# Columns of their own for the low parts' sums: five matmuls a block in place of six

## The chip, the cores and the metric

The kernel runs on one core of one Trainium2 chip. The metric is device time in microseconds (us) of one launch, taken as the median of the runs. Its engines appear below as PE (TensorE matmuls), PEld (TensorE weight loads), DVE (VectorE), ACT (ScalarE), POOL (GpSimd) and SP (SyncE, which here starts the transfers).

## The reference

The kernel computes one step of a decoder layer for 512 tokens of a prompt and 8 samples of one token each, 520 tokens in all, with 1024 features. Cut to its products:

```
h      = rmsnorm(x) * (1 + scale) + shift
proj   = h @ w_in                        # 1024 -> S5 input u | z | xBC | dt | gate_s5 | gate_ssd
ya     = gelu(s5(u));  ya = ya * sigmoid(ya @ w_glu + b_glu)
yb     = rmsnorm(ssd(conv(xBC), dt) * silu(z))          # 2048 features
merged = sigmoid(gate_s5) * (ya @ w_branch_s5) + sigmoid(gate_ssd) * (yb @ w_branch_ssd)
x     += gate * rmsnorm(merged @ w_out)
h      = rmsnorm(x) * (1 + scale_f) + shift_f
g, v   = split(h @ w_ffn_in)             # 2 x 2816
x     += gate_f * rmsnorm((silu(g) * v) @ w_ffn_out)
```

It also returns the new states of both state-space branches and of the convolution. All data are float32.

## The kernel before

Features lie on the partitions and tokens in the columns. A weight tile gives 128 output features. The 520 tokens are two halves of 260 (HT), since a PSUM bank holds 512 columns of sums. The input's 1024 features are 8 blocks of 128 (bssd has 16 blocks, fo has 22).

To keep the precision, each operand is held as a high and a low part, both of the type float32r (the profile's fp32r). A block is then three products: high by high and low input by high weights, and high input by low weights. `product` (L1148) issues them for a block, six matmuls of 260 columns into the tile's PSUM pair:

```
1152        for n in halves:
1154            self.mm(p[n][:, :s.stop - s.start], wh, xh[:, s], start=start, stop=False)
1155            self.mm(p[n][:, :s.stop - s.start], wh, xl[:, s], start=False, stop=False)
```

and then, for both halves, the high input with `wl`. Each matmul loads its 128 x 128 weights anew.

The main stream goes through the weight tiles in the order u, dt, gates, B, C, xs, z, then glu (8 tiles), bs5 (8), bssd (8), wo, fg and fu (gate and value of the second branch, 22 each), fo (8). wo and the first four fg and fu go by halves of the tokens, and so do the last two fo; the other 18 fg and 18 fu and the first six fo take both halves at once. The tiles use two PSUM pairs, pm0 and pm1, in turn. Four further banks serve the side work (the S5 and SSD branches, norms, states).

When a tile's sums are complete, `evac` (L1376) takes them out of pm: fg by a SiLU on ACT, fu by a product on DVE with the SiLU's result and a split in high and low part (ACT cast, DVE subtraction), fo by `mix_in` (L1561) with ACT, the others by copies, sigmoids and products. The weights for a tile two ahead are split meanwhile: ACT casts `whi`, DVE subtracts into `wlo`; of both there are three buffers in turn. From about 845 us on, the side work `ssd_state` renews the 8 samples' states: loads (in_ssm), products on DVE, stores.

No operation is issued at once. Every helper (`mm` L716, `acp` L694 for ACT copies, `vtt` L639 for DVE products and sums, `dma` L712) records an operation with an estimated cost in a `Plan`, which then searches for a good order by list scheduling with some random tries. All matmuls thus have line 722, all DVE products line 640, all ACT copies line 696. DVE and ACT take their operations strictly in the order found.

The end of the kernel: the last two fo tiles by halves (cut at 264 tokens, `cutp`), the last deviations in `rstd_last` (L1645, 256 tokens with a token a partition), `finish` (L1621) for the output.

Of the kernel before, what the change touches and what calls it, by code (L numbers as in the profile page):

```python
# [16 lines left out]
NP, NS = 512, 8  # L17
T = NP + NS
HT = T // 2
KD = 8  # L20
# [29 lines left out]
class Root:  # L50
    """A tile: `get` gives the real one (it may be made late); `loc` names the memory it lies in."""
# [14 lines left out]
class Ap:  # L66
    """A view of a tile: its shape and addresses at once, the real view when the operation is issued."""
# [110 lines left out]
# delay in us from the end of an operation to the start of one that waits for it  # L178
# [7 lines left out]
class Line:  # L186
    """The time of one engine: busy stretches, into whose gaps operations are put."""
# [24 lines left out]
class Plan:  # L212
    """Records operations with the memory they touch, and orders them for the engines."""
# [51 lines left out]
    def remake(self, loc, fn, words):  # L265
        """The memory `loc` gets a new tile: after everything that used the old one."""
# [8 lines left out]
    def order(self):  # L275
        """The best of some schedules: by the longest way to the end, then by latest starts."""
# [38 lines left out]
    def back(self):  # L315
        """Priorities from the schedule played backwards: the time from an operation's latest start to the end."""
# [35 lines left out]
    def play(self):  # L352
        """The course of the operations, each engine taking the most urgent of those that can start."""
# [69 lines left out]
    def shift(self, t, free, cand):  # L423
        """An operation of DVE that ACT may take at time t, where that is done sooner."""
# [32 lines left out]
class Arena:  # L457
    """One run of words in a tile of one type; blocks are cut out of it first fit."""
# [39 lines left out]
class Mem:  # L498
    """A fixed float32 arena, and slots whose type (float32 or float32r) is chosen when one is empty."""
# [10 lines left out]
    def find(self, n, dt, top):  # L510
        """The place for n words: an arena index (0 = the fixed one), or None."""
# [89 lines left out]
class Builder:  # L601
    def __init__(self, tc, I, O, sb, ps, dr):
# [10 lines left out]
        self.cutp = HT  # L613
# [6 lines left out]
        self.sg, self.ffh, self.ffl = {}, [], []  # L620
# [57 lines left out]
    def relu(self, o, a, s):  # L678
        """max(a + s, 0)"""
# [18 lines left out]
    def dma(self, o, a, boost=0.0):  # L698
        """Starts a transfer; returns the estimate of its end."""
# [25 lines left out]
    def idle(self, o, n, after=None):  # L725
        """Matmuls on zeros."""
        z = self.hi[:, KD - 1]
# [4 lines left out]
    def tp(self, o, a, n):  # L732
        d = self.ident[:n, :n]
        self.pe(.108, lambda: self.nc.tensor.transpose(real(o), real(a), real(d)), [o], [a, d])  # L734
# [8 lines left out]
    def bunch(self):  # L743
        """Matmuls that have to follow one another (sums that are open in one bank)."""
# [10 lines left out]
    def main(self):  # L755
        """The matmuls gathered in `group`, as one operation of the main stream."""
# [24 lines left out]
    def can(self, sizes, dt=F32, spare=0):  # L781
        """Whether the blocks fit, with room for `spare` token rows beside them."""
# [13 lines left out]
    def wblk(self, sizes, spare=2, dt=F32, prio=2):  # L796
        """Blocks for side work; a request that waits holds back those of less urgent work."""
# [88 lines left out]
    def ahead(self, j, table, f):  # L886
        """Prepares the weights of the use j of a chunk, unless that is done."""
# [3 lines left out]
    def split(self, hi, lo, src):  # L891
# [8 lines left out]
    def build(self):  # L900
# [4 lines left out]
        self.hi, self.lo = [rt(KD * T, n).rearrange("p (k t) -> p k t", k=KD) for n in ("hi", "lo")]  # L905
# [22 lines left out]
        # weight stream  # L928
# [30 lines left out]
        # half of the tokens at a time where the next step waits for all features  # L959
# [15 lines left out]
        # startup: modulation for the mixer, first norm  # L975
# [36 lines left out]
        # the first three tiles advance with the scale, two feature blocks at a time  # L1012
        b23 = [self.banks.pop() for _ in range(2)]
        ps = [[self.pm[0][:, n] for n in both], [self.pm[1][:, n] for n in both], b23]
        if NDUM:
            # matmuls on zeros: they keep the array busy, and so its clock at the full rate, until there are data
            self.mset("G", f_(self.hi[:, KD - 1]), 0.0)
            self.idle(b23[1], NDUM)
        for k in range(KD):
# [24 lines left out]
            for i in range(3):  # L1044
                self.product(*self.wt[i][:2], k, ps[i], both, k == 0, k == 7, self.hi[:, k], self.lo[:, k])
# [24 lines left out]
        for ti, (kind, idx, chs, m, halves) in enumerate(tiles[3:]):  # L1070
# [4 lines left out]
            else:  # L1075
                if self.nhalf == 0:
                    while len(self.banks) < 2:
                        self.tick()
                        self.now += 0.3
                    self.ring4 = [self.pm[0][:, 0], self.banks.pop(), self.pm[1][:, 0], self.banks.pop()]  # L1080
                if kind == "fo" and idx == 8 - NLAST and halves[0] == 0:
                    self.evac(*pend)
                    pend = None
                    self.cutp = T - 256
# [7 lines left out]
            nk, rhs = self.rhs(kind)  # L1092
            for k in range(nk):
# [8 lines left out]
                else:  # L1102
                    self.product(hi, lo, kk, pn, halves, k == 0, k == nk - 1, *rhs(k))
                if (kind, idx) == last:
                    if k == 0:
                        self.gelu()
                    self.split(self.hi[:, k], self.lo[:, k], self.ub.v(KD, T)[:, k])
                if (kind, idx) == ("glu", 7) and k < 7:
# [3 lines left out]
                    self.split(self.hi[:, k], self.lo[:, k], self.ub.v(KD, T)[:, k])  # L1112
                if (kind, idx) == ("bssd", 7):
                    self.ygh[k].free()
                    self.ygl[k].free()
# [28 lines left out]
    def span(self, n):  # L1144
        """The tokens of half n."""
        return slice(n * self.cutp, n * T + (1 - n) * self.cutp)

    def product(self, hi, lo, k, p, halves, start, stop, xh, xl):  # L1148
# [3 lines left out]
        for n in halves:  # L1152
            s = self.span(n)
            self.mm(p[n][:, :s.stop - s.start], wh, xh[:, s], start=start, stop=False)
            self.mm(p[n][:, :s.stop - s.start], wh, xl[:, s], start=False, stop=False)
        for n in halves:
            s = self.span(n)
            self.mm(p[n][:, :s.stop - s.start], wl, xh[:, s], start=False, stop=stop)
        self.main()

    def dt_mm(self, k, p, w):
        """The 32 columns of dt, high and low parts side by side, summed later."""
        self.group = []
        for n in range(2):
            for i, x in enumerate((self.hi, self.lo)):
                self.mm(p[:64, n, :HT], w[:, 64 * k:64 * k + 64], x[:, k, n * HT:(n + 1) * HT],
# [6 lines left out]
    def rhs(self, kind):  # L1173
        if kind == "bssd":
            return 16, lambda k: (self.ygh[k].v(T), self.ygl[k].v(T))
        if kind == "fo":
            return KFF, lambda k: (self.ffh[k].v(T), self.ffl[k].v(T))
        return KD, lambda k: (self.hi[:, k], self.lo[:, k])

# [1324 lines left out]
```

## Time and profile before

| what | us |
|---|---|
| time, median of 3 runs | 1202.06 (1200.11 to 1204.35) |
| profiled execution: span, first to last instruction | 1193.2 |
| PE busy | 1168.8 (98%) |
| DVE busy | 814.7 (68%) |
| ACT busy | 576.3 (48%) |

The profiled execution's time outside its span isn't recorded; the median of the runs is 8.9 us above the span. A window's row gives the busy time of each engine in a stretch of the span, the granted TensorE clock as a share of 2.4 GHz, and how busy the DMA engines were. A timeline row begins with the start of an instruction and its duration; matmuls overlap, so a matmul's price in a row of them is the distance from one start to the next and not the duration.

### The profile page before, as it was taken

The numbers are of one execution on the slowest core, as the hardware profiler recorded it, in microseconds if no ns is written. First come the engines' busy times: TensorE is split into PE (matmuls) and PEld (weight loads), VectorE is DVE, ScalarE is ACT, GpSimd is POOL, SyncE is SP. The second block draws the span as 40 slices with busy tenths as digits, with TensorE's granted clock in tenths as the row PEclk, the third lists the DMA queues.
The fourth block names the chain that finished last, engine by engine and source line by source line (L and its number), as shares of the span: only waits on it lengthen the run. The fifth ranks groups of instructions, "written<-read, shape, count | busy, mean of one in ns | idle before, by whom it ended". The sixth has DMA issues, their size and how long they took to land.

```text
span 1193.2 us, 24814 instructions
## 1 busy us (share of the span) xinstructions
PE 1168.8 (98%) x10182; PEld 1124.5 (94%) x10182; DVE 814.7 (68%) x1651; ACT 576.3 (48%) x981; POOL 4.9 (0%) x32
## 2 busy tenths in 40 slices
PE   8999999999999999999999999999999899999998
PEld 6899898999999999999998989999999899999997
DVE  6898989997696877868885435499576673322236
ACT  6655444357487657847853323465223222222233
POOL 0000000000000000000000000000000000000000
PEclk9999999999999999999999999999999999999999
DMA  8838698667243343355545674344566663223244
GB/s 292 278 119 219 162 215 224 180 160 208 82 134 101 114 128 125 116 175 169 188 145 201 241 268 144 129 166 147 182 217 203 198 206 104 88 81 97 83 130 135
DMA packets 118066, 195.49 MB, mean 164 GB/s; under 512 B 45856, under 2 KB 68800, under 8 KB 115648
## 3 DMA queue, kind: packets, MB, share of 16 engines
q1 hardware_dynamic: 117952, 193.90, 52.9%
q8 instruction: 80, 1.31, 0.4%
q14 instruction: 34, 0.28, 0.1%
HBM read 165.81 MB, written 23.86 MB: 159 GB/s over the span
## 4 chain that ended last, share of the span: by engine, by line
PE 79%; DMA 9%; DVE 7%; issue 1%; SPq 1%; ACT 1%; DVEq 0%; ACTq 0%
PE pm L722 64%; PE bank L722 14%; DVE s L640 4%; DMA arena<-in_ssm 3%; DVE arena L640 2%; PE bank L734 2%; DMA s<-in_w_as 1%; DMA out_ssm_s<-arena 1%; SPq L712 1%; DVE wlo L640 1%; DMA s<-in_w_in 1%; DMA ud<-s 1%; DMA s<-s 1%; DVE s L663 1%; ACT s L696 0%
## 5 line engine op out<-in xcount | busy, mean ns | idle before, releaser
L722 PE MATMUL pm<-hi,whi 128*128 128x260 f32 (+1 forms) x1856 | 497.5, 289 | 5.9 <-DVE arena L640 3.7
L722 PE MATMUL pm<-lo,whi 128*128 128x260 f32 (+1 forms) x1856 | 483.4, 282 | 0.0
L722 PE MATMUL pm<-hi,wlo 128*128 128x260 f32 x1840 | 370.4, 283 | 0.0
L722 PEld LDWEIGHTS pm<-hi,whi 128*128 128x128 f32 (+1 forms) x1856 | 349.6, 188 | 17.4 <-issue 13.0
L722 PEld LDWEIGHTS pm<-lo,whi 128*128 128x128 f32 (+1 forms) x1856 | 349.1, 188 | 0.1
L640 DVE TENSOR_TENSOR wlo<-arena,whi 128x1024 fp32r<-128x1024 f32 (+1 forms) x157 | 188.8, 1203 | 146.7 <-ACT whi L696 144.9
L722 PEld LDWEIGHTS pm<-hi,wlo 128*128 128x128 f32 x1840 | 282.9, 188 | 0.0
L696 ACT CAST whi<-arena 128x1024 fp32r<-128x1024 f32 (+1 forms) x158 | 162.6, 1029 | 197.1 <-PE pm L722 180.2
L722 PE MATMUL pm<-s,whi 128*128 128x260 f32 (+2 forms) x1128 | 184.2, 283 | 0.0
L640 DVE TENSOR_TENSOR arena<-arena 128x512 f32<-128x512 f32 (+11 forms) x299 | 140.3, 494 | 49.8 <-DMA arena<-in_ssm 29.4
L722 PEld LDWEIGHTS pm<-s,whi 128*128 128x128 f32 x1128 | 156.2, 188 | 5.1 <-issue 4.2
L722 PE MATMUL pm<-s,wlo 128*128 128x260 f32 (+2 forms) x564 | 117.2, 283 | 0.0
L722 PEld LDWEIGHTS pm<-s,wlo 128*128 128x128 f32 x564 | 88.1, 188 | 0.0
L691 ACT ACT_TABLE_LOAD x63 | 80.8, 1283 | 10.3 <-DMA s<-acd 3.5
L722 PE MATMUL bank<-s,s 128*64 128x128 f32 (+5 forms) x672 | 75.8, 282 | 5.6 <-ACT s L696 4.4
L722 PEld LDWEIGHTS bank<-s,s 128*128 128x128 f32 (+2 forms) x672 | 61.3, 164 | 10.9 <-ACT s L696 5.3
L691 ACT ACTIVATE s<-s 128x520 f32<-128x520 f32 (+10 forms) x89 | 50.0, 570 | 38.3 <-DVE s L640 17.7
L691 ACT ACTIVATE arena<-pm 128x260 f32<-128x260 f32 (+3 forms) x44 | 21.2, 489 | 92.7 <-PE pm L722 85.7
L640 DVE TENSOR_TENSOR s<-arena,s 128x520 fp32r<-128x520 f32 (+5 forms) x60 | 56.5, 948 | 10.6 <-ACT s L696 10.4
L640 DVE TENSOR_TENSOR s<-s,arena 128x8 f32<-128x8 f32 (+6 forms) x138 | 48.6, 369 | 13.8 <-ACT s L691 12.7
L722 PE MATMUL bank<-hi,s 128*128 128x260 f32 x256 | 55.5, 285 | 0.0
L722 PE MATMUL pm<-hi,s 128*128 128x260 f32 x256 | 55.0, 285 | 0.0
(122 smaller groups left out, 1265.8 us busy)
## 6 DMA issues: line engine op xcount, KB each, us to landing
arena<-in_w_in SPq DMA_DIRECT2D x59, 512.0 KB, 3.7
arena<-in_w_fi SPq DMA_DIRECT2D x44, 512.0 KB, 4.4
arena<-in_w_ada SPq DMA_DIRECT2D x12, 1024.0 KB, 7.5
arena<-in_w_fo SPq DMA_DIRECT2D x20, 512.0 KB, 3.6
arena<-in_ssmT SPq DMA_DIRECT2D x16, 512.0 KB, 4.4
s<-acd SPq DMA_DIRECT2D x16, 512.0 KB, 4.3
arena<-in_w_bssd SPq DMA_DIRECT2D x16, 512.0 KB, 5.4
arena<-in_ssm SPq DMA_DIRECT2D x32, 256.0 KB, 3.8
```

The source lines that it names most:

```text
L640: self.op("V", .068 + self.fs(o) / 960, lambda: self.nc.vector.tensor_tensor(out=real(o), in0=real(a), in1=real(b), op=op), [o], [a, b, *a ...
L663: self.op("V", .068 + self.fs(o) / 960, lambda: self.nc.vector.tensor_tensor_scan(out=real(o), data0=real(a), data1=real(b), initial=0.0, ...
L691: self.op("A", c, lambda: self.nc.scalar.activation(real(o), real(a), f, bias=real(bias), scale=real(scale)), [o], [a, scale, bias], None ...
L696: self.op("A", c, lambda: self.nc.scalar.copy(real(o), real(a)), [o], [a])
L712: p = self.op("S", .475 if same else .65, lambda: self.nc.sync.dma_start(out=real(o), in_=real(a)), [o], [a], None, c)
L722: self.pe(c, lambda: self.nc.tensor.matmul(real(o), lhsT=real(l), rhs=real(r), start=start, stop=stop), [o], [l, r])
L734: self.pe(.108, lambda: self.nc.tensor.transpose(real(o), real(a), real(d)), [o], [a, d])
```

## The change

In the tiles of glu, bs5, bssd, whole fg and fu, and whole fo (`WIDE`; 66 tiles, called wide here), the high and the low part of the input lie side by side in one tile, `xhl`: for each half 260 high columns and then 260 low ones. A block's product with the high weights is now, for each half, one matmul of 348 columns (260 high, and the first LA = 88 low ones), which writes 348 columns of pm, and one matmul of 344 for the remaining 172 low columns of both halves, which writes into a side bank of its own, `lob`. The two matmuls with the low weights stay. The sums of high and low input thus stand apart, and `evac` adds them.

```
 def product(self, hi, lo, k, p, halves, start, stop, x, wide=False, flush=True):
         wh, wl = [a[:, 128 * k:128 * k + 128] for a in (hi, lo)]
         self.group = []
+        if wide:
+            w = HT + LA
+            for n in halves:
+                self.mm(p[n][:, :w], wh, x[:, n].rearrange("p c t -> p (c t)")[:, :w], start=start, stop=False)
+            for n in halves:
+                self.mm(p[n][:, :HT], wl, x[:, n, 0], start=False, stop=stop)
+            self.late.append((self.lob[:, :2 * (HT - LA)].rearrange("p (a t) -> p a t", a=2), wh, x[:, :, 1, LA:], start, stop))
+            if flush:
+                for o, w, r, f, l in self.late:
+                    self.mm(o, w, r, start=f, stop=l)
+                self.late = []
...
+                    self.product(hi, lo, kk, pn, halves, k == 0, k == nk - 1, rhs(k), wide,
+                                 k > (0 if (kind, idx) in (last, ("glu", 7), ("bssd", 7)) else 1))
...
     def evac(self, kind, i, p, halves):
         pv = p[:, :, :HT] if len(halves) == 2 else None
+        if len(halves) == 2 and kind in WIDE:
+            lb = self.mblk(T)
+            l2 = sp(lb.v(T))
+            self.acp(l2[:, :, LA:], sp(self.lob[:, :2 * (HT - LA)]))
+            self.acp(l2[:, :, :LA], p[:, :, HT:HT + LA])
+            self.vtt(l2, l2, pv, ADD)
+            pv = l2
+            p = l2
...
     def mm(self, o, l, r, start=True, stop=True):
-            c = max(n / 2400, .111) if m > 32 else .048
+            c = max(n / 2400 + (.0114 if n < 300 else .0025), .112) if m > 32 else .048
-            c = max(n * 4 / 2400, .216) * max(m, 32) / 128 + (.021 if m <= 64 else 0.0)
+            c = max(n * 4 / 2400 + .005, .224) * max(m, 32) / 128 + (.021 if m <= 64 else 0.0)
...
     def rstd_last(self):
+        at = [(c0, 128), (c0 + 128, 128), (T - 128, HT - 256)]
-            for j in range(2):
-                o = c0 + 128 * j
+            for j, (o, _) in enumerate(at):
                 self.mm(q[:, j:j + 1], s.v(T)[:, o:o + 128], self.ones[:, 0:1])
...
         self.vts(d[:, 0], self.ident, t[:, 2, 0:1], MULT)
         self.act(d[:, 1], self.ident, AF.Copy, scale=t[:, 2, 1:2])
+        self.vts(d[:, 2], self.ident, t[:, 2, 2:3], MULT)
```

Around it: there is one `lob`, one of the four side banks, held until the tiles by halves reuse it. The 344-column matmuls of a tile's first two blocks are kept back until the third (`late`), before which `lob` must have been emptied. The splits, the SSD operands (`ygp`) and fu's results (`ffp`) write into the new layout; fg, fu and fo read the summed block `lb` instead of pm. `cutp` is gone: the last two fo tiles have halves of 260 and 260, and `rstd_last` makes the last 260 deviations in three pieces. `tp` and the costs in `mm` are new numbers for the planner.

PE's row in the whole fg and fu tiles, where a new tile begins. hi, lo and xhl are the input, whi and wlo the weights' parts, pm the tile's sums, bank_68 the side bank. Before:

```order
L722 MATMUL pm_69<-hi,wlo_76 128x260 x2
L722 MATMUL pm_70<-hi,whi_71 128x260
L722 MATMUL pm_70<-lo,whi_71 128x260
L722 MATMUL pm_70<-hi,whi_71 128x260
L722 MATMUL pm_70<-lo,whi_71 128x260
L722 MATMUL pm_70<-hi,wlo_74 128x260 x2
```

After:

```order
L724 MATMUL pm_70<-xhl,whi_72 128x348 x2
L724 MATMUL pm_70<-xhl,wlo_75 128x260 x2
L724 MATMUL pm_70<-xhl,whi_72 128x348 x2
L724 MATMUL pm_70<-xhl,wlo_75 128x260 x2
L724 MATMUL pm_70<-xhl,whi_72 128x348 x2
L724 MATMUL pm_70<-xhl,wlo_75 128x260 x2
L724 MATMUL bank_68<-xhl,whi_72 128x344 x3
L724 MATMUL pm_70<-xhl,whi_72 128x348 x2
L724 MATMUL pm_70<-xhl,wlo_75 128x260 x2
L724 MATMUL bank_68<-xhl,whi_72 128x344
```

The side bank is first written behind the twelfth matmul of the tile; from there on each block has five.

ACT's row in the same stage, from one SiLU of fg to the next. Before:

```order
L691 ACTIVATE arena<-pm_69 128x520
L696 CAST whi_72<-arena 128x1024
L696 CAST whi_73<-arena 128x1024
L696 CAST s_54_8728<-arena 128x520
L691 ACTIVATE arena<-pm_69 128x520
```

After:

```order
L693 ACTIVATE arena<-arena 128x520
L698 COPY arena<-bank_68 128x2x172
L698 COPY arena<-pm_70 128x2x88
L698 CAST whi_72<-arena 128x1024
L698 CAST s_59_9012<-arena 128x2x260
L698 COPY arena<-bank_68 128x2x172
L698 COPY arena<-pm_69 128x2x88
L698 CAST whi_73<-arena 128x1024
L693 ACTIVATE arena<-arena 128x520
```

Two copies head each tile's work, ahead of the cast of the next weights; the conversion of fu's result (s) stands behind that cast and ahead of the next tile's copies.

DVE's row there. Before, from one product out of pm to the next (wlo the weights' low part, 128x512 the states' products, s the split of fu's result):

```order
L640 TENSOR_TENSOR arena<-arena,pm_70 128x520
L640 TENSOR_TENSOR arena<-arena 128x512
L640 TENSOR_TENSOR wlo_75<-arena,whi_72 128x1024
L640 TENSOR_TENSOR s_56_8803<-arena,s_56_8803 128x520
L640 TENSOR_TENSOR arena<-arena 128x512 x4
L640 TENSOR_TENSOR wlo_76<-arena,whi_73 128x1024
L640 TENSOR_TENSOR arena<-arena 128x512 x3
L640 TENSOR_TENSOR arena<-arena,pm_70 128x520
```

After, from one addition out of pm_70 to the next:

```order
L642 TENSOR_TENSOR arena<-arena,pm_70 128x520
L642 TENSOR_TENSOR arena<-arena 128x520
L642 TENSOR_TENSOR wlo_75<-arena,whi_72 128x1024
L642 TENSOR_TENSOR s_54_8604<-arena,s_54_8604 128x2x260
L642 TENSOR_TENSOR arena<-arena 128x512 x4
L642 TENSOR_TENSOR arena<-arena,pm_69 128x520
L642 TENSOR_TENSOR wlo_76<-arena,whi_73 128x1024
L642 TENSOR_TENSOR arena<-arena 128x512 x3
L642 TENSOR_TENSOR arena<-arena,pm_70 128x520
```

DVE read pm once for two tiles and reads it in both now; states' products stand ahead of each of these additions.

## Rows read from the trace of the kernel before

**Rows 1.** The page: span, busy time by engine, chain that ended last

```profile
span 1193.2 us, 24814 instructions
...
PE 1168.8 (98%) x10182; PEld 1124.5 (94%) x10182; DVE 814.7 (68%) x1651; ACT 576.3 (48%) x981; POOL 4.9 (0%) x32
...
PE 79%; DMA 9%; DVE 7%; issue 1%; SPq 1%; ACT 1%; DVEq 0%; ACTq 0%
```

**Rows 2.** Windows: stretch, length, PE, PEld, DVE, ACT, POOL busy, clock, DMA, GB/s

```profile
9.00:16.00 7.00, 5.67 (x75) 4.42 (x68) 5.36 (x23) 4.73 (x15) 0.00 (x0) 1.00 0.97 326
...
132.00:133.50 1.50, 1.50 (x9) 1.50 (x8) 1.44 (x4) 0.78 (x2) 0.00 (x0) 0.50 0.78 231
...
569.00:632.80 63.80, 63.80 (x621) 60.06 (x612) 53.89 (x110) 46.21 (x68) 0.00 (x0) 1.00 0.52 166
...
845.00:1054.00 209.00, 204.87 (x1710) 204.48 (x1709) 118.87 (x155) 56.66 (x72) 0.00 (x0) 1.00 0.52 164
1054.00:1149.00 95.00, 95.00 (x794) 95.00 (x793) 25.20 (x33) 24.20 (x43) 0.00 (x0) 1.00 0.31 92
```

**Rows 3.** Timeline, TensorE: first matmuls of two blocks of an fg or fu tile

```profile
900.57 0.28 PE L722 MATMUL pm<-hi,whi 128*128 128x260 f32 x1
...
901.29 0.28 PE L722 MATMUL pm<-hi,whi 128*128 128x260 f32 x1
```

**Rows 4.** Timeline, TensorE at the half clock, five matmuls apart

```profile
132.25 0.42 PE L722 MATMUL pm<-hi,whi 128*128 128x260 f32 x1
...
133.33 0.42 PE L722 MATMUL pm<-lo,whi 128*128 128x260 f32 x1
```

**Rows 5.** Timeline, TensorE: 512 and 260 columns, first after a 32-column group

```profile
12.02 0.50 PE L729 MATMUL bank<-hi 128*128 128x512 f32 x1
12.36 0.28 PE L722 MATMUL bank<-hi,whi 128*128 128x260 f32 x1
...
15.23 0.39 PE L722 MATMUL pm<-hi,whi 128*128 128x260 f32 x1
15.45 0.28 PE L722 MATMUL pm<-lo,whi 128*128 128x260 f32 x1
```

**Rows 6.** The dt tile's 64-column weights: timeline, and groups of weight loads

```profile
72.61 0.28 PE L722 MATMUL pm<-lo,whi 128*64 128x260 f32 x1
...
74.04 0.28 PE L722 MATMUL pm<-lo,whi 128*64 128x260 f32 x1
...
L722 PEld LDWEIGHTS pm<-lo,whi 128*128 128x128 f32 x1840 | 347.0, 189 | 0.1
...
L722 PEld LDWEIGHTS pm<-lo,whi 128*64 128x64 f32 x16 | 2.2, 135 | 0.0
```

**Rows 7.** Groups on ACT and DVE: total us, mean ns of one, idle before

```profile
L696 ACT COPY s<-bank 128x512 f32<-128x512 f32 x19 | 11.0, 586 | 4.6 <-DVE s L640 2.4 <-PE bank L734 1.1 <-PE bank L722 1.0
L696 ACT COPY s<-bank 128x128 f32<-128x128 f32 x17 | 4.5, 265 | 16.3 <-PE bank L722 13.6 <-DVE s L640 2.5
...
L640 DVE TENSOR_TENSOR arena<-arena,pm 128x520 f32<-128x520 f32 x31 | 21.5, 692 | 45.2 <-PE pm L722 45.1
```

**Rows 8.** Waits from 845 to 965: total us, times, longest

```profile
DVE arena L640 <- DMA arena<-in_ssm: 26.2, 14, 5.0
...
ACT s L696 <- DVE arena L640: 15.9, 6, 5.6
```

**Rows 9.** Timeline of the longest wait of TensorE in that stage

```profile
952.48 1.42 DVE L640 TENSOR_TENSOR arena<-arena 128x512 f32<-128x512 f32 x2 [3.85 <-DMA arena<-in_ssm]
...
953.82 0.69 DVE L640 TENSOR_TENSOR arena<-arena,pm 128x520 f32<-128x520 f32 x1
...
954.65 0.36 PE L722 MATMUL pm<-hi,whi 128*128 128x260 f32 x1 [3.67 <-DVE arena L640]
```

**Rows 10.** Timeline after the last fo matmul: scaling in the last deviations

```profile
1184.34 0.29 DVE L646 TENSOR_SCALAR arena<-arena 128x128 f32<-128x128 f32 x1
```

**Rows 11.** Timeline, TensorE: 48 matmuls of 73 columns

```profile
261.50 5.47 PE L722 MATMUL bank<-s,s 128*128 128x73 f32 x48
```

More of the change, by code (lines that the diff above doesn't have):

```diff
@@ L19 @@
 HT = T // 2
+LA = 88
+WIDE = ("glu", "bs5", "bssd", "fg", "fu", "fo")
 KD = 8
@@ L889, in ahead, with split @@
             f(self.uses[j])
-    def split(self, hi, lo, src):
+    def split(self, hl, src, halves=(0, 1)):
+        hi, lo = [hl[:, c] if len(halves) == 1 else hl[:, :, c] for c in (0, 1)]
+        if len(halves) == 2:
+            src = src.rearrange("p (a t) -> p a t", a=2)
         self.acp(hi, src)
@@ L1044, in build @@
             for i in range(3):
-                self.product(*self.wt[i][:2], k, ps[i], both, k == 0, k == 7, self.hi[:, k], self.lo[:, k])
+                self.product(*self.wt[i][:2], k, ps[i], both, k == 0, k == 7, self.hl[:, k])
                 self.tick()
@@ L1076, in build @@
                 if self.nhalf == 0:
-                    while len(self.banks) < 2:
+                    while not self.banks:
                         self.tick()
                         self.now += 0.3
-                    self.ring4 = [self.pm[0][:, 0], self.banks.pop(), self.pm[1][:, 0], self.banks.pop()]
+                    self.ring4 = [self.pm[0][:, 0], self.lob, self.pm[1][:, 0], self.banks.pop()]
                 if kind == "fo" and idx == 8 - NLAST and halves[0] == 0:
@@ L1092, in build @@
             nk, rhs = self.rhs(kind)
+            wide = len(halves) == 2 and kind in WIDE
+            if wide and self.lob is None:
+                while not self.banks:
+                    self.tick()
+                    self.now += 0.3
+                self.lob = self.banks.pop()
             for k in range(nk):
@@ L1106, in build @@
                         self.gelu()
-                    self.split(self.hi[:, k], self.lo[:, k], self.ub.v(KD, T)[:, k])
-                if (kind, idx) == ("glu", 7) and k < 7:
+                    for i in (k - 1,) * (k > 0) + (k,) * (k == 7):
+                        self.split(self.hl[:, i], self.ub.v(KD, T)[:, i])
+                if (kind, idx) == ("glu", 7):
                     if k == 0:
@@ L1111, in build @@
                         pend = None
-                    self.split(self.hi[:, k], self.lo[:, k], self.ub.v(KD, T)[:, k])
+                    else:
+                        self.split(self.hl[:, k - 1], self.ub.v(KD, T)[:, k - 1])
                 if (kind, idx) == ("bssd", 7):
-                    self.ygh[k].free()
-                    self.ygl[k].free()
+                    for i in (k - 1,) * (k > 0) + (k,) * (k == 15):
+                        self.ygp[i].free()
                 if (kind, idx) == ("u", NA - 1):
@@ L1144, in span, with product @@
     def span(self, n):
-        return slice(n * self.cutp, n * T + (1 - n) * self.cutp)
-    def product(self, hi, lo, k, p, halves, start, stop, xh, xl):
+        return slice(n * HT, n * HT + HT)
+    def product(self, hi, lo, k, p, halves, start, stop, x, wide=False, flush=True):
         wh, wl = [a[:, 128 * k:128 * k + 128] for a in (hi, lo)]
         self.group = []
[L1152 to L1158, printed above, removed]
+        if wide:
[9 more added lines that the diff above has]
+                self.late = []
+        else:
+            for n in halves:
+                for c in range(2):
+                    self.mm(p[n][:, :HT], wh, x[:, n, c], start=start and c == 0, stop=False)
+            for n in halves:
+                self.mm(p[n][:, :HT], wl, x[:, n, 0], start=False, stop=stop)
         self.main()
@@ L1164, in dt_mm @@
         for n in range(2):
-            for i, x in enumerate((self.hi, self.lo)):
-                self.mm(p[:64, n, :HT], w[:, 64 * k:64 * k + 64], x[:, k, n * HT:(n + 1) * HT],
+            for i in range(2):
+                self.mm(p[:64, n, :HT], w[:, 64 * k:64 * k + 64], self.hl[:, k, n, i],
                         start=(k + i == 0), stop=(k + i == 8))
@@ L1521, in evac @@
                     self.spawn(self.boosted(self.finish(n), (H0, 0.0)[n]), 0)
+        if lb:
+            lb.free()
     @staticmethod
```

105 lines of the change are left out of this document (56 added, 49 removed).

## The prediction

> **What bounds the kernel now.** I read the busy shares and the chain of work that ended last first. TensorE is busy for 1168.8 of 1193.2 us, and it holds 79% of the chain [rows 1]. Then I read the windows by stage. In the stages that the change touches TensorE is busy without a break, or nearly: 63.80 of 63.80 us at the end of the glu tiles and in the bs5 tiles, 204.87 of 209.00 in the whole fg and fu tiles, 95.00 of 95.00 in the first six fo tiles, at a granted clock of 1.00 [rows 2]. So there the time is the number of matmuls times what one takes in a row of them; whatever else moves counts only if it makes TensorE wait. In those windows 95.00 us hold 794 matmuls, 119.6 ns each, and 204.87 us hold 1710, 119.8 ns each; I use 119.7. The timeline says the same of one block: from 900.57 to 901.29 its six matmuls take 0.72 us [rows 3].
>
> The clock alone does not explain 119.7. 260 columns at 2.4 GHz are 108.3 ns, so each matmul carries 11.4 ns more. The whole forecast hangs on where these 11.4 ns come from, since the change streams the same columns (per block 6 x 260 = 1560 before, 2 x 348 + 2 x 260 + 344 = 1560 after) in one matmul less. It does so in 676 blocks: 64 of glu, 64 of bs5, 128 of bssd, 288 of fg and fu, 132 of fo.
>
> **The matmuls.** Before, a block takes 6 x 119.7 = 718.2 ns. After, two matmuls of 260 keep their 119.7 and three have a width that the stages of before do not have. I bound those from both sides.
>
> - The cheap end: no excess at all. At half the clock there is none: between 132.25 and 133.33 five matmuls of 260 take 1.08 us, 216 ns each, and 260 / 1.2 is 216.7 [rows 2, 4]. Then 348 columns take 145.0 ns and 344 take 143.3, a block 2 x 145.0 + 2 x 119.7 + 143.3 = 672.7, and 45.5 x 676 = 30.8 us go.
> - The dear end: the excess grows with the columns. One matmul of 512 columns of the same type ran at the full clock [rows 2, 5]: it starts at 12.02 and the next starts at 12.36, 0.34 us. It stands first behind a group of 32-column matmuls. A 260-column matmul in the same place, at 15.23, is followed at 15.45, after 0.22. (The rows have two decimals; the starts behind them are 340 and 224 ns apart.) So 252 further columns took 116 ns, 0.46 ns a column, where 2.4 GHz gives 0.417. From 119.7 at 260 this gives 119.7 + 88 x 0.46 = 160.2 ns for 348 and 119.7 + 84 x 0.46 = 158.3 for 344. A block is 320.4 + 239.4 + 158.3 = 718.1: nothing is saved.
>
> Between these ends I take the dear one, because it is the only row with a wide matmul of this type, and because the two causes that could end with the matmul have rows against them. If the weight load set the pace, short weights would help. The dt tile's weights have 64 columns, their loads take 135 ns in the records instead of 189, and yet from 72.61 to 74.04 twelve matmuls take 1.43 us, 119.2 ns each [rows 6]. If it were a fixed price per matmul, it would show at half the clock too, or 512 columns would have cost 105 ns more and not 116. What remains is a stream that yields about 2.2 columns per ns however the clock would allow 2.4. Term: **0.0 us**, between -30.8 and 0.
>
> [...]
>
> **The sums' own columns.** A wide tile leaves 344 columns in one side bank and 2 x 88 behind the 260s. Their evacuation adds two ScalarE copies and one VectorE addition for each of 66 tiles. By the copies of 128 and 512 columns (265 and 586 ns, [rows 7]) 344 columns take 0.45 us and 176 take 0.31; the addition is the 692 ns of [rows 7]. All of it lies beside TensorE as long as three covers hold.
> The side bank is single. The order shows that its first matmul of a tile stands behind the third block, after twelve matmuls into the pm bank: 3 x (2 x 160.2 + 239.4) = 1679 ns. The copy of 0.45 us, first in ScalarE's row at the tile's end, fits in with 1.2 us over. Cost 0 if ScalarE is free.
> The pm banks are double. The evacuation ends 0.45 + 0.31 + 0.69 = 1.45 us later, against a tile of 8 x 718 = 5.75 us. Cost 0.
> VectorE has room on the mean: in the densest of the wide stages it is busy for 53.89 of 63.80 us [rows 2], and eleven additions bring 7.6 us, 61.5 together. That is close. If it runs over, the next work in its row is the preparation of bssd's operands, of which the last are needed by the sixteenth block of that stage, 15 x 0.72 = 10.8 us into it, so I take nothing, with 2 us in the upper end.
> Where the covers fail is known from before. Between 845 and 965 VectorE waited 26.2 us in 14 places for the old states from memory [rows 8]. Once that reached TensorE: VectorE's product out of pm stood in its row behind a state product that had waited 3.85 us, began at 953.82, and TensorE went on at 954.65 after 3.67 us idle [rows 9]. Before, VectorE reads pm in every second tile of this stage (fu), since fg goes through ScalarE. After, it reads pm in every tile. Twice as many places for the same accident would be one more of 3.7 us; but the new order is a new draw, which may as well have none. I take the middle, **+1.9 us**, between 0 and four times 3.7.
>
> **The rest.** The last deviations are made in three pieces instead of two: one more 128 x 128 scaling like the 0.29 us at 1184.34 [rows 10], on the chain after the last matmul: **+0.3 us**. The last half tiles have 260 columns in place of 264 and 256: the same sum, 0. The planner's new prices of matmuls take no time; they change the order, and that is inside the bounds of the term above. Splits write high and low parts to another place with the same sizes: 0. Transfers stay as they are, and no queue is passed by a step.
>
> Sum: 0.0 + 1.9 + 0.3 = +2.2. The profiled span of 1193.2 us becomes 1195.4. The page gives no time of that execution outside its span, so I set the 8.9 us between 1193.2 and the median of the runs, 1202.06, on top unchanged: **1204.3 us**.
>
> **The rivals.**
>
> *The excess ends with the matmul's length (A).* Forty-eight matmuls of only 73 columns take 5.47 us, 114 ns each at most [rows 11]: with full weights a matmul takes no less, and so a load of 128 columns sets a floor near 112. 260 columns at 108.3 lie just under it, and two streams of nearly one length may hinder each other; 344 and 348 columns, at 143.3 and 145.0, lie far over it. For it: both the half clock, where there is no excess, and the floor. Against it: the 64-column weights and the 512-column row. Priced from no excess (30.8 us saved) to half of it (5.7 ns a matmul: 150.7 and 149.0, a block 689.8, 19.2 us saved), in the middle 25.0: 1202.06 - 25.0 + 2.2 = **1179.3 us**, from 1173.5 to 1185.1.
> [...]
>
> *A fixed price per matmul (B).* Each keeps its 11.4 ns: 156.4 and 154.7, a block 706.9, 11.3 x 676 = 7.6 us saved, 1202.06 - 7.6 + 2.2 = **1196.7 us**, from 1194 to 1203. For it: the same 11.4 in every stage. Against it: 512 columns.
>
> *VectorE's row holds TensorE up (D), which ends slower.* The place is the whole fg and fu tiles from 845 on, while the states are renewed. Each addition out of pm stands behind whatever state product waits for its transfer, up to 5.0 us a time [rows 8], and ScalarE, which waited 15.9 us there for VectorE in six places, holds the copies of the side bank behind such a wait. It decides from the point where such a wait outlasts what is left of the tile. Three hits of 3.7 us more than in the forecast: 1204.3 + 11.1 = **1215.4 us**. Against it: only one of 14 waits did so before, and the copies stand ahead of the waiting conversion in their own tile.
>
> **How the numbers follow.** The forecast (columns set the price) gets 0.40, A 0.34, B 0.13, D 0.13. About 0.3% (3.6 us) is what a measurement of this kernel can tell from no change: faster means below 1198.5, slower above 1205.7. The forecast's own range is 1201 to 1211, by 0 to 8 us of waits where the sum has 1.9, and by 0.455 ns a column at the lower end (159.7 and 157.9, a block 716.8, 0.9 us saved); it is split into 0.02 faster, 0.25 same, 0.13 slower. A is faster. B is 0.10 faster, 0.03 same. D is slower. So faster 0.46, same 0.28, slower 0.26: the likeliest single case is no change, though the cases that are faster hold more together than it does. The range must take in A and the forecast: from 1175 (A's largest savings left out, 0.04) to 1211 (most of D left out, 0.11).
>
> **What would show it.** In the changed kernel's timeline, a block of fo tiles: if 348 columns take 158 to 161 ns and five matmuls about 718, the forecast's reading holds; at 145 to 151, A; near 156, B. The windows of the whole fg and fu tiles must then show the same or more us, with TensorE's idle time there at 4 to 8 us against 4.1 before (209.00 less 204.87), released by VectorE or ScalarE. The additions must stand at about 0.69 us, the copies at 0.45 and 0.31. It is wrong above all if a wide matmul comes out under 155 ns, because then the one row of 512 columns, on zeros and at a group's edge, did not speak for the rest.

## The result, and the profile after

The changed kernel takes 1213.9 us (median; 1210.26 to 1215.67) where the one before takes 1201.1: a ratio of 1.0108, 95% interval 1.0083 to 1.0134. It is slower by 12.8 us, 2.9 us above the upper end of my range.

The page of the changed kernel, as in [rows 1]:

```profile
span 1212.0 us, 23699 instructions
...
PE 1182.9 (98%) x9512; PEld 1133.4 (94%) x9512; DVE 852.5 (70%) x1699; ACT 614.1 (51%) x1129; POOL 5.3 (0%) x32
...
PE 66%; DMA 18%; DVE 10%; ACT 3%; issue 2%; SPq 1%; DVEq 0%; ACTq 0%
```

The profiled span grew by 18.8 us, from 1193.2 to 1212.0, and that is more than the medians grew: this execution took 1213.99 us, 2.0 us more than its span. So the 8.9 us that I set outside the span of before were hardly all outside it; with 2.0 us its profiled execution would have taken about 1195, an estimate, some 6 us under its median.

TensorE issues 670 instructions less, and yet it is busy for 14.1 us more. Its idle time (span less busy) grew from 24.4 to 29.1 us. The third number is in the cores' view, the mean granted clock. Before, and after:

```profile
core 0: 1193.2 us, clock 0.998
```

```profile
core 0: 1212.0 us, clock 0.989
```

Span times what is missing to 1 is the time that the half clock took away, at most, since part of it falls on idle time: 2.4 us before and 13.3 after. Idle time and lost clock together make 4.7 + 10.9 = 15.6 of the 18.8 us.

This pair overstates the clock's part. Over the 101 executions of the kernel before that were timed beside the experiments below, the clock is 0.993 on the mean and 8.2 us are lost to it; over the four of the changed kernel it is 0.989, and 13.6 us. So the clock makes some 5 of the 12.8 us. Span times clock, what would be left at the full clock, is 1190 and 1198 us in these means, and 1190.8 and 1198.7 in the two profiles: some 8 us are idle time and work.

The matmuls are not to blame. The first six fo tiles of the changed kernel, in a window as in [rows 2], and a block in the timeline (start, duration):

```profile
1070.00:1168.00 98.00, 98.00 (x685) 98.00 (x684) 29.92 (x40) 29.75 (x56) 0.00 (x0) 1.00 0.32 91
```

```profile
1099.72 0.48 PE L724 MATMUL pm<-s,whi 128*128 128x348 f32 x2
1100.04 0.40 PE L724 MATMUL pm<-s,wlo 128*128 128x260 f32 x2
1100.28 0.32 PE L724 MATMUL bank<-s,whi 128*128 128x344 f32 x1
1100.44 0.48 PE L724 MATMUL pm<-s,whi 128*128 128x348 f32 x2
```

Two matmuls of 348 columns take 0.32 us, two of 260 take 0.24, one of 344 takes 0.16: 0.72 for the block, as before. By the window, 98.00 / 685 x 5 = 715 ns against 718. From the start of the whole fg and fu tiles to the last fo half (the 121st to the 181st subtraction of a weight's low part on VectorE) both kernels need 317 us, 317.0 and 317.1.

Most of the loss lies far ahead of the tiles that the change is about: before 300 us the changed kernel idles 1.8 us more and loses some 10 us more to the clock, of the 15.6 in all. The stretch from 60 to 300 us, where the gates and the first B, C, xs and z tiles run beside the S5 branch, first before and then after:

```profile
60.00:300.00 240.00, 230.94 (x2033) 224.80 (x2033) 214.73 (x473) 123.07 (x270) 2.94 (x20) 0.99 0.73 186
```

```profile
60.00:300.00 240.00, 228.82 (x1955) 222.60 (x1955) 211.52 (x462) 116.69 (x264) 2.81 (x19) 0.96 0.68 176
```

No tile there is wide, but TensorE issues 78 matmuls less in the same 240 us and has a clock of 0.96. One place shows how. TensorE, ScalarE and VectorE of the changed kernel from 266 on, and windows of 2 us:

```profile
266.72 0.68 DVE L642 TENSOR_TENSOR s<-s 128x512 f32<-128x512 f32 x1
...
267.08 0.66 PE L736 MATMUL bank<-arena 128*128 128x128 f32 x4
...
267.32 0.67 DVE L642 TENSOR_TENSOR s<-s,s 128x496 f32<-128x496 f32 x1
...
267.44 0.20 ACT L659 COPY s<-s 128x8 f32<-128x8 f32 x1 [2.32 <-DVE s L642]
...
268.34 1.03 ACT L698 CAST whi<-arena 128x1024 fp32r<-128x1024 f32 x1
...
269.27 0.58 ACT L698 COPY s<-bank 128x512 f32<-128x512 f32 x1
...
269.90 9.19 PE L724 MATMUL bank<-s,s 128*128 128x72 f32 x48 [2.16 <-ACT s L698]
...
278.84 1.21 PE L724 MATMUL pm<-xhl,whi 128*128 128x260 f32 x4
```

```profile
268.00:270.00 2.00, 0.10 (x1) 0.10 (x1) 2.00 (x3) 1.98 (x4) 0.00 (x0) 1.00 0.44 96
270.00:272.00 2.00, 2.00 (x16) 2.00 (x17) 2.00 (x4) 1.08 (x3) 0.00 (x0) 0.85 0.90 193
272.00:274.00 2.00, 2.00 (x12) 2.00 (x11) 1.93 (x5) 0.34 (x2) 0.00 (x0) 0.50 0.95 318
...
278.00:280.00 2.00, 2.00 (x11) 2.00 (x11) 2.00 (x3) 0.40 (x1) 0.00 (x0) 0.50 0.53 108
280.00:282.00 2.00, 2.00 (x13) 2.00 (x12) 1.97 (x4) 0.00 (x0) 0.00 (x0) 0.59 0.61 140
282.00:284.00 2.00, 2.00 (x19) 2.00 (x18) 1.97 (x4) 0.00 (x0) 0.00 (x0) 1.00 0.92 197
```

The order has transposes for the S5 branch (L736), then 48 narrow matmuls (72 and 73 columns) that need ScalarE's copy of them, with not one matmul of the main stream between. The copy stands behind a cast and starts at 269.27; TensorE idles for 2.16 us. From about 271 to 282 its granted clock is 0.50, and then 1.00 again, though TensorE is busy all the while. The wait costs 2 us, and the half clock behind it about 5 (0.57 on the mean from 270 to 282). The kernel before has such stretches too, but fewer: a window of 1.50 us at 0.50 stands in [rows 2].

Between 300 and 860 us, where among others the wide tiles of glu, bs5 and bssd lie, the changed kernel idles 5.1 us more; in the whole fg and fu tiles (860 to 1070) it idles 2.6 us less.

### The profile page after: what moved, and what is told of

Read it like the earlier page. It is cut to its first block, busy times and chain, and to the rows that moved or that the text cites. A ratio compares the mean times of both kernels' runs of the same rounds, so it can differ in the third digit from the quotient of the medians.

```text
span 1212.0 us, 23699 instructions
## 1 busy us (share of the span) xinstructions
PE 1182.9 (98%) x9512; PEld 1133.4 (94%) x9512; DVE 852.5 (70%) x1699; ACT 614.1 (51%) x1129; POOL 5.3 (0%) x32
## 4 chain that ended last, share of the span: by engine, by line
PE 66%; DMA 18%; DVE 10%; ACT 3%; issue 2%; SPq 1%; DVEq 0%; ACTq 0%
PE pm L724 46%; PE bank L724 18%; DMA out_ssm_s<-arena 4%; DMA arena<-in_ssm 4%; DVE arena L642 4%; DVE s L642 3%; DMA s<-in_w_as 2%; DVE wlo L642 2%; DMA ud<-s 1%; PE bank L736 1%; DVE s L653 1%; SPq L714 1%; ACT s L698 1%; DMA s<-s 1%; DMA s<-in_w_in 1%
## 5 line engine op out<-in xcount | busy, mean ns | idle before, releaser
L724 PE MATMUL pm<-xhl,whi 128*128 128x260 f32 (+2 forms) x2880 | 543.8, 300 | 2.0 <-DVE arena L642 1.4
L724 PEld LDWEIGHTS pm<-xhl,whi 128*128 128x128 f32 (+1 forms) x2880 | 422.9, 190 | 13.3 <-issue 9.1
L724 PE MATMUL pm<-xhl,wlo 128*128 128x260 f32 x1840 | 372.0, 284 | 0.0
L724 PEld LDWEIGHTS pm<-xhl,wlo 128*128 128x128 f32 x1840 | 301.2, 189 | 0.0
L642 DVE TENSOR_TENSOR arena<-arena 128x512 f32<-128x512 f32 (+10 forms) x300 | 150.3, 520 | 57.5 <-DMA arena<-in_ssm 29.4
L724 PE MATMUL pm<-s,whi 128*128 128x348 f32 (+1 forms) x608 | 143.0, 319 | 0.5 <-DVE s L653 0.5
L724 PE MATMUL bank<-xhl,whi 128*128 128x344 f32 (+1 forms) x448 | 121.9, 318 | 0.0
L724 PE MATMUL pm<-s,wlo 128*128 128x260 f32 x564 | 117.4, 283 | 0.9 <-DVE wlo L642 0.9
L724 PE MATMUL bank<-s,whi 128*128 128x344 f32 (+1 forms) x348 | 95.0, 311 | 0.2 <-ACT arena L698 0.2
L724 PEld LDWEIGHTS bank<-xhl,whi 128*128 128x128 f32 x448 | 77.7, 189 | 1.7 <-issue 1.4
```

Source lines behind the costliest of these rows:

```text
L642: self.op("V", .068 + self.fs(o) / 960, lambda: self.nc.vector.tensor_tensor(out=real(o), in0=real(a), in1=real(b), op=op), [o], [a, b, *a ...
L724: self.pe(c, lambda: self.nc.tensor.matmul(real(o), lhsT=real(l), rhs=real(r), start=start, stop=stop), [o], [l, r])
```

## The experiments

**The price of a matmul by its width.** Matmuls of one form in rows of 24, put behind the end of the kernel before:

```
+        for n in (260, 128, 192, 224, 260, 300, 348, 400, 448, 512):
+            for i in range(24): mm(i, v(520 * (i % 4), n), n)
+        # then, 24 each: 344 in two runs of 172; 348 from column 1 on; every second of 1024; 260
```

> The kernel before with 336 further matmuls at its end, of float32r, in rows of 24 of one form each: 128 to 512 columns, then 344 in two runs of 172, 348 from a start that is one column off, 512 columns with every second one taken, and 260 again. They only measure; the outputs are those of before. Columns set the price (forecast): a start every 2.4 + 0.451 ns a column, 119.7 at 260, 137.7 at 300, 159.4 at 348, 182.8 at 400, 233.3 at 512; under 224 columns the weight load's 108 to 112. [...] Rival B: N / 2.4 + 11.4, so 156.4 and 224.7. [...]

One execution, 1256.5 us with the rows. Windows cut at the start of each row of 24: 128, 260, 348 and 512 columns, 344 in two runs, 348 one column off, and 512 with every second taken. (The counts take in matmuls that reach over an edge.)

```profile
1199.26:1201.89 2.63, 2.63 (x26) 2.63 (x25) 0.00 (x0) 0.00 (x0) 0.00 (x0) 1.00 0.00 0
...
1207.30:1210.15 2.85, 2.85 (x27) 2.85 (x25) 0.00 (x0) 0.00 (x0) 0.00 (x0) 1.00 0.00 0
...
1213.49:1217.33 3.84, 3.84 (x27) 3.84 (x26) 0.00 (x0) 0.00 (x0) 0.00 (x0) 1.00 0.00 0
...
1226.57:1232.14 5.57, 5.57 (x26) 4.50 (x24) 0.00 (x0) 0.00 (x0) 0.00 (x0) 1.00 0.00 0
1232.14:1235.94 3.80, 3.80 (x26) 3.80 (x24) 0.00 (x0) 0.00 (x0) 0.00 (x0) 1.00 0.00 0
1235.94:1239.82 3.88, 3.88 (x27) 3.88 (x25) 0.00 (x0) 0.00 (x0) 0.00 (x0) 1.00 0.00 0
1239.82:1250.67 10.85, 10.85 (x27) 4.97 (x25) 0.00 (x0) 0.00 (x0) 0.00 (x0) 1.00 0.00 0
```

Each length over 24: 110, 119, 160, 232, 158, 162 and 452 ns. From 260 to 512 columns the price is 0.45 ns a column; rivals A (145 to 151 at 348) and B (156 there, and 225 at 512) are out. 128 columns cost 110, at a floor that 192 and 224 columns share (113 each). The last form tells more of what is paid for: 512 columns, every second one and so over twice the memory, cost 452 ns in place of 232, so the price does not go by the number of columns alone; it fits the memory that a matmul passes over. Counted in columns passed over, taken or not, it is 119 / 260 = 0.46, 160 / 348 = 0.46, 232 / 512 = 0.45 and 452 / 1024 = 0.44 ns a column; a start one column off costs 1.7 ns more. Only one stride was run, so a price of the stride itself stays possible. Either way fewer and wider matmuls save next to nothing, as the sum had it: 715 against 718 ns is 2 us over the 676 blocks, an estimate.

**Which edit changed the early order.** The planner's prices of matmuls alone, put into the kernel before; and taken out of the changed kernel; and the changed kernel without wide tiles.

```
 def mm(...):                                  # e1: these and tp, in the kernel before
-    c = max(n / 2400, .111) if m > 32 else .048
+    c = max(n / 2400 + (.0114 if n < 300 else .0025), .112)
-    c = max(n * 4 / 2400, .216) * max(m, 32) / 128 + ...
+    c = max(n * 4 / 2400 + .005, .224) * max(m, 32) / 128 + ...
                                               # e2: the same backwards, in the changed kernel
-WIDE = ("glu", "bs5", "bssd", "fg", "fu", "fo")
+WIDE = ()                                     # e3; the side bank is then taken where the tiles by halves begin
```

(The first new line ends at .112; the condition that stands behind it in the diff ahead is not in the kernel.)

> The kernel before, with only the planner's new prices of matmuls and transposes. Theory (the new order lost it: the search for an order found one in which TensorE waits in the first 300 us and its clock falls): any edit of the prices is a new draw, so this is off the 1201 us of before by 3 to 15 us, slower, with a mean granted clock under 0.995. Rival 1 (the evacuation and the side bank of the wide tiles cost it): 1201, within 3 us. Rival 2 (the new prices mislead the search): 1210 or more.

> The changed kernel with the planner's old prices. Theory: another draw, between 1201 and 1215, its distance from 1201 made by idle time and lost clock before 600 us, while from the whole fg and fu tiles on it needs the same 317 us as both others. Rival 1: stays at 1214, within 3. Rival 2: back to 1201, within 3.

> The changed kernel with no wide tile: new layout, new prices, cuts and deviations, but six matmuls of 260 a block and no evacuation of a side bank. Theory: another draw, 1201 to 1215, 317 us from the whole fg and fu tiles on. Rival 1: 1201, within 3 us. Rival 2: 1210 or more.

e1: 1216.2 us, ratio 1.0141 (1.0110 to 1.0173). The kernel before becomes as slow as the changed one by nothing but numbers that no engine ever sees. e2: 1199.5, ratio 0.9994 (0.9978 to 1.0011). e3: 1229.3, 1.0236 (1.0207 to 1.0266), with all of the change but the wide tiles. Rival 1, the evacuation, is out. Rival 2, the prices, met its range all three times. My theory, that each edit is a new draw, missed its own: e1 by under 1 us, e2 by 1.5, e3 by 14, and e3 needs 328.9 us where I had 317. But three draws could still have come out so.

**A draw or the prices.** The search starts its random tries from a seed, 149 in both kernels. Other seeds, one line each:

```
-SEED = 149
+SEED = 1        # b_seed1, b_seed2: kernel before; a_seed1: changed; c_seed1: changed, old prices
```

> The kernel before with the search's random seed 1 in place of 149, nothing else. Theory (every edit that touches the search is a new draw of the order, and 149 is a good one for the old prices): 3 to 25 us over before, by idle time and lost clock before 300 us and in the whole fg and fu tiles. Rival 2 (the new prices mislead the search, the old ones do not): within 4 us of before, since the prices are the old ones.

> The kernel before with seed 2. As with seed 1: theory 3 to 25 us over before and not the same as seed 1; rival 2 within 4 us of before.

> The changed kernel with its new prices and seed 1. Theory: another draw, as likely under 1214 us as over it, in the same spread as the seeds of before (1200 to 1225). Rival 2: 1212 us or more, since the prices are the new ones.

> The changed kernel with the old prices and seed 1. Theory: a draw like the others, 1200 to 1225; 1199.5 at seed 149 was one of them. Rival 2: within 4 us of 1200, since the prices are the old ones.

b_seed1 1197.4 (0.9975, 0.9960 to 0.9991), b_seed2 1196.8 (0.9972, 0.9954 to 0.9990), a_seed1 1213.9 (1.0108, 1.0077 to 1.0139), c_seed1 1190.8 (0.9920, 0.9894 to 0.9946). The seeds spread by some us, and the old prices stay low and the new ones high. My theory of the draw fell; rival 2 held, but for c_seed1, which is 9 us under its 1200 where 4 were allowed. c_seed1 beats both kernels.

**Why the new prices harm.** By the trace the new price of 260 columns is the true one (0.1197) and the old one 7% too low. (Those of the wide matmuls stayed too low: 147.5 ns for 348 columns and 145.8 for 344, where the trace has 160 and 158. A wide block is 680 ns in the plan and 715 on the chip.) That gave a new theory: with a price that is too low the planner puts more of the main stream between a piece of side work and the matmul that waits for it, a margin against whatever takes longer on the chip than in the plan. The rival: the prices of float32 matmuls and transposes do the harm.

```
 g1: the changed kernel, float32r price old           g2: float32 and transpose prices old
 g3: all prices new;  def add(...):
+        if eng != "P":
+            cost, xfer = 1.08 * cost, 1.08 * xfer    # and the hand-over delays times 1.08
 g5: all prices new;  def order(self):
+        for o in ops:
+            if o.eng == "P":
+                o.cost /= 1.08
```

> The changed kernel, seed 149, with only the price of float32r matmuls (the main stream) back to the old one: 0.111 us at 260 columns, where the new one is 0.1197 and the trace says 0.1197. Margin theory (the old price lets the planner think that the main stream runs 7% faster than it does, so it puts more of it between a piece of side work and the matmul that waits for it; with the true price that margin is gone): 1190 to 1203. Rival 3 (the prices of float32 matmuls and transposes mislead it): 1210 to 1217.

> The changed kernel, seed 149, with only the prices of float32 matmuls and transposes back to the old ones; the main stream keeps its true price. Margin theory: stays at 1208 to 1220. Rival 3: 1190 to 1203.

> The changed kernel with all its new prices, seed 149, and for the planner every duration and delay that is not TensorE's taken 1.08 times as long (VectorE, ScalarE, GpSimd, transfers, hand-overs). Margin theory: the ratio counts and not the price itself, so the margin is back, 1190 to 1204, with less idle time of TensorE and a higher mean clock before 300 us than the changed kernel (282.80 us busy of 300, clock 0.96). Rival 4 (the old price itself helps by chance, through the order it leads to): no better than 1210.

> The changed kernel with its new prices while the operations are recorded, and for the search of the order all of TensorE's prices divided by 1.08. Margin theory, if the margin works in the search: 1190 to 1204. If it works in the recording, where the builder's clock decides when side work is begun and which memory it gets: 1208 to 1220.

g1 1204.5 (1.0029, 1.0009 to 1.0049), g2 1204.5 (1.0037, 1.0018 to 1.0056), g3 1200.5 (0.9995, 0.9977 to 1.0013), g5 1200.0 (0.9997, 0.9985 to 1.0010). g3 and g5 leave every new price and only shift TensorE's prices against all others; the loss is gone. g5 says that it is in the search. g1 missed its range by 1.5 us and g2 by 3.5 on the other side: either set of prices makes up most of the loss, so it is not the main stream's price alone that counts, as I had it, but TensorE's as a whole. Rival 3 missed both of its ranges too.

The stretch from 60 to 300 us in g3, against the two above:

```profile
60.00:300.00 240.00, 231.88 (x2026) 226.52 (x2025) 213.99 (x468) 122.70 (x265) 3.35 (x21) 0.98 0.72 185
```

2026 matmuls again, as 2033 before, with 1955 in the changed kernel. So the ratio of the prices is what counts. That it works as a margin of main stream in front of each waiting matmul was not read from the orders, and one place speaks against so simple a picture: e1 has a block of the main stream (six matmuls from 265.43) between such transposes and the narrow matmuls, and still waits:

```profile
265.43 0.36 PE L722 MATMUL pm<-hi,whi 128*128 128x260 f32 x1
...
268.52 0.67 PE L722 MATMUL bank<-s,s 128*128 128x72 f32 x4 [2.13 <-ACT s L696]
```

**At another seed, without wide tiles, and with more of it.**

```
 h1: the changed kernel, WIDE = (), old prices        h2: the kernel before, new prices, SEED = 1
 h3: g3 with SEED = 1                                 h4: the changed kernel, old prices, SEED = 1, but
+    c = max(n / 2580, .103) if m > 32 else .048
```

> The changed kernel without wide tiles (six matmuls of 260 a block, no side bank's evacuation), with the planner's old prices, seed 149. It tells what the wide product alone is worth: columns set the price, so 719.4 less 716.1 ns a block, 1 to 2 us. Expected 1196 to 1206, within 5 us of the same kernel with wide tiles (1199.5 at seed 149), and far under the 1229 of the narrow kernel with new prices. If the wide product itself lost or won more, it is off by over 6 us.

> The kernel before with the new prices and seed 1. Margin theory: the true prices cost at this seed too, 1208 to 1225 (1197.4 with the old prices at this seed). If seed 149 with new prices (1216) was only a bad draw: 1195 to 1205.

> The changed kernel with all its new prices, seed 1, and every duration and delay that is not TensorE's taken 1.08 times as long in the plan. Margin theory: 1188 to 1203, against 1213.9 without that margin. If the 1200.5 of seed 149 was a good draw: 1205 to 1216.

> The changed kernel, seed 1, old prices but the main stream's lower still (0.103 us at 260 columns, 14% under what the trace shows). If more margin is better, under 1190.8; if the old price had enough of it, 1188 to 1200; if too much of it spreads the side work past its due times, over 1200.

h1 1200.1 (1.0006, 0.9993 to 1.0020), h2 1219.4 (1.0167, 1.0144 to 1.0189), h3 1198.5 (0.9998, 0.9975 to 1.0020), h4 1209.6 (1.0080, 1.0062 to 1.0099). h1 to h3 went as the margin theory had it, and h4 shows its other side: too low a price costs as well, there in the first tiles (the 29th subtraction of a weight's low part at 73.3 us, at 57.3 in c_seed1).

**Whether the fastest one was a draw.** The changed kernel with old prices at two more seeds:

> The changed kernel with the old prices, seed 2. 1190 to 1203: with the margin every seed so far gave 1190.8 to 1204.5. Under 1195 would say that the 1190.8 of seed 1 was the wide tiles' and not one draw's; 1197 or more that it was a draw.

> The changed kernel with the old prices, seed 3. As with seed 2.

c_seed2 1195.7 (0.9968, 0.9950 to 0.9986), c_seed3 1195.8 (0.9973, 0.9957 to 0.9989). Both are faster than before, but not as fast as 1190.8: part of that was the draw.

All medians, in us, in pairs:

```
seed, what                  old prices   new prices   prices cost
149, six matmuls (before)     1200.3       1216.2        15.9
149, six, new layout          1200.1       1229.3        29.2
149, wide tiles               1199.5       1213.9        14.4
1, six matmuls (before)       1197.4       1219.4        22.0
1, wide tiles                 1190.8       1213.9        23.1
```

The runs of a row are in part from different series, in which the kernel before came to 1199.4 to 1201.1. The new prices cost 14 to 29 us in every row. The wide tiles, against six matmuls in the kernel before, save 0.8 and 6.6 us with old prices and 2.3 and 5.5 with new ones, but with old prices that is no more than seeds differ: the changed kernel has 1195.5 on the mean of four seeds, the kernel before 1198.1 on three, and at seed 2 they are 1.1 apart. In the new layout the wide tiles save 0.6 us with old prices and 15.4 with new ones. This fits their price: where a block is six matmuls, priced rightly, the stretch of 317 us from the whole fg and fu tiles on takes 326.2 in e1, 328.9 in e3 and 325.5 in h2 (with old prices 316.1 in b_seed1, 317.5 in b_seed2, 317.3 in h1); where it is wide, priced 5% too low, it stays at 317.1 and, in a_seed1, 317.3. No run gave the wide matmuls their true price. Part of that stretch, before and in e1:

```profile
870.00:1060.00 190.00, 185.87 (x1552) 185.48 (x1551) 104.09 (x135) 50.59 (x64) 0.00 (x0) 1.00 0.51 161
```

```profile
870.00:1060.00 190.00, 184.11 (x1506) 183.40 (x1505) 107.97 (x142) 51.05 (x64) 0.00 (x0) 0.98 0.54 167
```

And one sum moves little: span less idle less lost clock is 1166.4 us before, 1169.6 after, 1167.7 in e1, 1170.3 in e3, 1166.9 in g3, 1165.7 in c_seed1, 1173.2 in c_seed2. Among these TensorE's work changes by 7.5 us at most; the kernels differ more in how long it idles and in how long it runs at half the clock. Two far ends, e3 and c_seed2:

```profile
core 0: 1228.4 us, clock 0.984
```

```profile
core 0: 1192.4 us, clock 0.999
```

e3 loses 38.4 us to idling (1228.4 less 1190.0 busy) and 19.7 to the clock, c_seed2 18.0 and 1.2. (Other executions of c_seed2 have a lower clock, 0.9955 on the mean of ten.)

## Why the prediction was wrong

- **The matmuls: right.** 160.2 and 158.3 ns forecast, 160 and 158 measured; the block 715 where the sum had 718. That the one row of 512 columns [rows 5] spoke for all holds. Rivals A and B, which held 0.47 of the chances and all of those for faster but 0.02, are out.
- **The planner's prices: the step that failed.** The prediction said that they "take no time; they change the order, and that is inside the bounds of the term above". They cost 14.4 us at this seed (e2 against the changed kernel), nearly all of it outside the place where I had put that term. The bounds of that term, 0 to 14.8 us, would have held the loss, but the range took only 0 to 8 us of them, and for one stage. I had looked for waits where the change adds work, and not where the new order has another sequence of old work; the order's rows from 60 to 300 us could have been read before.
- **The term itself.** +1.9 us for VectorE's row in the whole fg and fu tiles. The waits there, as in [rows 8], from 860 to 1070 of the changed kernel:

```profile
DVE arena L642 <- DMA arena<-in_ssm: 27.0, 20, 2.8
...
PE pm L724 <- DVE arena L642: 1.4, 1, 1.4
```

  TensorE idles 1.4 us there for VectorE, less than the 3.7 before, and 1.6 in all, where the prediction's sign was 4 to 8, though VectorE still waits 27 us for the states. Rival D named the right sign and the wrong place; that its 1215.4 lies 1.5 us from the measured time is luck. Its mechanism is real in other orders: e3, with new prices and no wide tile, waits there 11.4 us in 5 places:

```profile
PE pm L724 <- DVE arena L642: 11.4, 5, 5.7
```

  and h1, the same with old prices, 1.7. The order decides it, not the additions.
- **The covers: right in size, and held but for 1.6 us.** The copies and the addition, as in [rows 7], 445, 311 and 691 ns where the sum had 0.45, 0.31 and 0.69:

```profile
L698 ACT COPY arena<-bank 128x344 f32<-128x344 f32 x54 | 24.1, 445 | 103.4 <-PE bank L724 100.9 <-issue 2.4
...
L698 ACT COPY arena<-pm 128x176 f32<-128x176 f32 x54 | 16.8, 311 | 0.7 <-PE pm L724 0.7
```

```profile
L642 DVE TENSOR_TENSOR arena<-arena,pm 128x520 f32<-128x520 f32 x54 | 37.3, 691 | 52.5 <-ACT arena L698 52.5
```

  That it makes TensorE wait nowhere in the fo tiles is in their window, 98.00 busy of 98.00. In the bssd tiles, where the prediction called VectorE's room close and took nothing, with 2 us in the upper end, TensorE waits 1.6 us in four places that are not there before, for weights, operands and once for the side bank (640 to 760):

```profile
PE pm L724 <- DVE wlo L642: 0.9, 1, 0.9
PE pm L724 <- DVE s L653: 0.5, 2, 0.3
PE bank L724 <- ACT arena L698: 0.2, 1, 0.2
```

- **The clock: missing.** The sum took every us of waiting at its own length and had no term for the half clock. By the means above the clock is some 5 of the 12.8 us, by the profiled pair 10.9 of 18.8; at the place shown, 2.16 us of waiting had about 5 us behind it.

What stays open: whether it is a margin at all, and what it guards against. g3 made every other duration and delay longer at once, so it doesn't tell whether transfers, ScalarE, VectorE or the hand-overs run longer on the chip than in the plan. And the spread of single orders (1190.8 to 1199.5 over four seeds of the changed kernel with old prices) was not explained order by order.

## What to carry to other kernels

Where a planner decides the order, a corrected price is an edit to every stage: compare the orders from the first row on, and time the prices alone before anything else is added to them. A wrong price may be doing work that nobody gave it; if it is put right, look for a factor with a place of its own that does the same, as the 1.08 on all other durations did here. And a wait of TensorE is to be read together with the clock behind it, which can cost more than the wait: about 5 us behind 2.16 us in the changed kernel, and nothing behind the 3.67 us of [rows 9], where the clock stays at 1.00 from 954.6 to 970.

## What the runs showed of the hardware

At the full clock float32r matmuls cost 0.45 ns a column from 260 to 512 columns (119 ns at 260, 160 at 348, 232 at 512), and 0.88 a column where every second one is taken (452 ns for 512). It did not scale with the clock: at 0.50 [rows 2] 260 columns needed 216 ns [rows 4], where twice 119 would be 238. With weights of 128 columns no row came under 110 ns a matmul (128, 192 and 224 columns nearly alike, 2.63, 2.71 and 2.70 us for 24); that the weight load sets this floor was not tested by itself.

TensorE's granted clock fell to 0.50 behind a wait of 2.16 us in the changed kernel and was back at 1.00 some 10 us later, with TensorE busy on narrow matmuls and the first of the main stream in between.
